# An MLP on one core: the residual's row of factors moves from the up projection to the down projection's first block

## The chip, the cores and the metric

The kernel runs on one core of a Trainium2 chip. The metric is the device time of one execution in microseconds. Engines: TensorE (PE) multiplies, VectorE (DVE), ScalarE (ACT) and GpSimd (POOL) work elementwise, SyncE (SP) issues all the DMAs of this kernel, and each of them works through its own queue in order.

## The reference

A decoder layer on 1024 tokens of width 1024: mixing heads, cross attention, then the part that matters here, an MLP with squared ReLU, and a last norm.

```python
u = jax.nn.relu(rmsnorm(x, ln2[l]) @ w_ff1[l])
x = x + (u * u) @ w_ff2[l]
return rmsnorm(x, ln_f)
```

`w_ff1` is 1024 x 4096, `w_ff2` 4096 x 1024. The kernel does not wait for this norm's factor r: it feeds the up projection with x times a factor c of each token that it has already (that of the norm before). Since relu(c a) squared is c squared times relu(a) squared, the MLP comes out too large by (c/r) squared. The last norm does not mind a factor of a whole token, once EPS is scaled too. So it is enough that the residual x is multiplied, token by token, by the same (c/r) squared, a row of 1024 factors called `inv`, before the down projection's sums are added to it.

## The kernel before, in words

Everything is held transposed: features on the 128 partitions, the 1024 tokens along the free axis, in two halves of 512. Each product of two fp32 numbers is made as three fp32r products (lines 184, 185, 186 in `mm3`) of a high part (`wh`, made by ScalarE, line 132) and a low part (`wl`, made by VectorE, line 133). TensorE's work in the MLP is two block algorithms of Strassen's kind, with seven products (numbers 1 to 7) instead of eight.

*Up projection* (about 880 to 1215 us of the profile). A list of jobs, one product of 12 matmuls each, runs over 16 pairs of tiles of `w_ff1`. A job takes a bank of PSUM from a cycle of eight, and the next job on the same bank waits until VectorE has added the sum to what stands in SBUF (line 1326). The squared results are combined and stored to DRAM (`right`, lines 1366 and 1367; `plain` for the last block). Between the jobs, by their number `at`: at 30 the factors `inv` are turned into a row (`to_row`: a transpose on TensorE, line 247, a copy by ScalarE, 248, a store to DRAM, 249, and a load that spreads it over all partitions, 251), in the constant tile `row`. From 32 on, every fourth job calls `stretch`: in turns it loads a 128x1024 piece of the residual from DRAM (`x2d`, line 1427) into a buffer `w4`, or multiplies that piece by `row` on VectorE (1430) and stores it back (1431). There are eight pieces. The last pairs of jobs use the halves of `row` as scratch afterwards. The tag `w4` has five buffers of 128x1024, shared by the pairs' partial results, the stretches and later by the down projection's split weights.

*Down projection* (about 1215 to 1500 us). 7 blocks of 4 steps, `(b, m)`. A step has seven products of 6 matmuls, on four banks: products 2, 4 and 3 go on in the banks of 1, 5 and 7, after VectorE has added those to the residual's tile `x2` (line 1517). `left` loads the raw weights of the next step (1403), GpSimd makes sums of them (1410), and ScalarE and VectorE split both (132, 133; the split of 128x768 goes to two `w4` buffers, that of 128x1024 to `wh` and `wl`). The residual's tiles are loaded once, tile m before or during step m - 1 of the first block (`x2_load`, 1476: 1 MB each), stay in SBUF over all blocks, and are prepared on GpSimd by two subtractions (`distances`, 1490).

The order of the instructions on every engine is set by a scheduler that plays the program through with costs of its own, so a change of dependences and buffers moves instructions.

Of the kernel before, what the change touches and what calls it, by code (L numbers as in the profile page):

```python
# [12 lines left out]
ALU = mybir.AluOpType  # L13
# [8 lines left out]
KT = D // P  # L22
# [22 lines left out]
def hybrid_layer(ctx: ExitStack, tc: tile.TileContext, a: dict, out: bass.AP):  # L45
    nc = tc.nc
    v, s, g = nc.vector, nc.scalar, nc.gpsimd
# [11 lines left out]
    def sb(tag, shape, bufs, dt=F32):  # L59
        return pool.tile(shape, dt, tag=tag, name=name(tag), bufs=bufs)  # L60

    def act(dt=F32R):
        return sb("act", [P, 8, TH], 7, dt)
# [8 lines left out]
    def w4(shape=(P, 1024), dt=F32):  # L72
        t = sb("w4", [P, 1024], 5, dt)[: shape[0]]
        return t.rearrange("p (a b) -> p a b", b=shape[2]) if len(shape) == 3 else t
# [33 lines left out]
    def const(n, shape, dt=F32):  # L108
        return pool.tile(shape, dt, tag=n, name=n, bufs=1)

    load = nc.sync.dma_start
# [76 lines left out]
    def both(pair, f):  # L188
        return f(pair[0]), f(pair[1])
# [52 lines left out]
    rowd = dram.tile([4, T], F32, name="rowd")  # L242

    def to_row(dst, cols, n, at, bank=None):

        ps = (bank or ov_)()
        nc.tensor.transpose(ps[:n, :P], cols, ident)
        s.activation(dst[:n, :P], ps[:n, :P], AF.Copy)
        load(at.rearrange("o (t q) -> (o t) q", t=n), dst[:n, :P])
        w = min(dst.shape[1], n * P)  # L250
        return load(dst, at[:, :w].broadcast_to([P, w]))

    row = const("row", [P, T])
# [12 lines left out]
    at = 0  # L266
# [33 lines left out]
    h = [(act(), act()), (act(), act())]  # L300
# [20 lines left out]
    for k in range(KT):  # L321
        if k == 2:
            load(wg_raw, a["w_gate"])
        if k % 2 == 0:
            c = slice(k % 4 * 256, k % 4 * 256 + 512)
# [354 lines left out]
    for _ in range(2):  # L680
        t = act().rearrange("p a b -> p (a b)").rearrange("p (i c) -> p i c", i=4)
# [363 lines left out]
    n = 0  # L1045
# [7 lines left out]
    for step in fill:  # L1053
        n, e = divmod(halves[0], 2)
# [82 lines left out]
    x2d = dram.tile([P, KT // 2, 2, 2, TH], F32, name="x2d")  # L1137
# [23 lines left out]
    def bank():  # L1161
        turn[0] += 1
        return ps_tile(cycle[turn[0] % 8])
# [63 lines left out]
    def prepare(at):  # L1227
        while prep and first[prep[0]] <= at + LEAD:
            left_up(*prep.pop(0))
# [10 lines left out]
    inv = gcol.rearrange("p a b -> p (a b)")[:, :8]  # L1240
# [10 lines left out]
    def norm_factors(hf):  # L1251

        ps = bank()
        sum_cols(ps[:, 0:4], accs[hf], 4)
        c = slice(4 * hf, 4 * hf + 4)
        v.tensor_scalar(out=inv[:, c], in0=ps[:, 0:4], scalar1=1.0 / D, scalar2=EPS, op0=ALU.mult, op1=ALU.add)
        for _ in range(2):
            v.tensor_tensor(out=inv[:, c], in0=inv[:, c], in1=rcol[:, c], op=ALU.mult)
# [110 lines left out]
    def put_right(b, k, pair):  # L1369

        u11, u12, u21, u22 = (pair.u[c] for c in ("11", "12", "21", "22"))
        t1 = pair.t1
        to = lambda c: [right[b][ORDER.index(c), :, p_, k] for p_ in range(2)]
        t = {}

        def one():
            sub(t1, u12, u11)
            put(to("11"), u11)

        def two():  # L1380
            x = w4()
            t[2], t[4] = x[:, :TH], x[:, TH:]
            sub(t[2], u22, t1)
            sub(u12, u22, u12, g)
            put(to("t1"), t1)

        def four():
            sub(t[4], t[2], u21)
            put(to("22"), u22)

        return [one, two, lambda: put(to("t3"), u12), four, lambda: put(to("21"), u21), lambda: put(to("t2"), t[2]), lambda: put(to("t4"), t[4])]

    def put_plain(k, pair):
        f = lambda i, hf: lambda: put([plain[2 * i + k, :, p_, hf] for p_ in range(2)], pair.u[f"{i + 1}{hf + 1}"])
        return [f(i, hf) for hf in range(2) for i in range(2)]
# [4 lines left out]
    def left(src):  # L1400

        q = sb("wr", [P, 1024], 2)
        after[0] = load(q, src)
        q = q.rearrange("p (q c) -> p q c", q=4)
        q21, q11, q12, q22 = (q[:, i] for i in range(4))
        sums = z4()[:, :1024].rearrange("p (q c) -> p q c", q=4)
        s1, s2, s3, s4 = (sums[:, i] for i in range(4))

        for o, x, y, op in ((s1, q21, q22, ALU.add), (s2, s1, q11, ALU.subtract), (s3, q11, q21, ALU.subtract), (s4, s2, q12, ALU.subtract)):
            g.tensor_tensor(out=o, in0=x, in1=y, op=op)  # L1410
        hq, lq = (w4(dt=F32R)[:, :768].rearrange("p (q c) -> p q c", q=3) for _ in range(2))
        split(hq, lq, q[:, 1:])
        hs, ls = (sb(t, [P, 1024], 3, F32R).rearrange("p (q c) -> p q c", q=4) for t in ("wh", "wl"))
        split(hs, ls, sums)
        f = lambda hi, lo, i: both((hi, lo), lambda t: t[:, i].rearrange("p (k c) -> p k c", k=2))
        return {1: f(hq, lq, 0), 2: f(hq, lq, 1), 3: f(hs, ls, 3), 4: f(hq, lq, 2), 5: f(hs, ls, 0), 6: f(hs, ls, 1), 7: f(hs, ls, 2)}

    stretches = list(range(KT))

    held = []  # L1420

    def stretch(n):

        x = x2d[:, n // 2, n % 2].rearrange("p h c -> p (h c)")
        if not held:
            held.append(w4())
            load(held[0], x)
        else:
            t = held.pop()
            v.tensor_tensor(out=t, in0=t, in1=row, op=ALU.mult)  # L1430
            load(x, t)

    pairs = {}
    later = []
    for at, (p_, i) in enumerate(jobs):
        prepare(at)
        for _ in range(2 if at < 2 else 1):
            if rest and at:
                rest.pop(0)()
        if at == 6:  # L1440
            norm_factors(1)
        if at == 30:
            to_row(row, inv, 8, rowd[3:4], bank)
        if at > 30 and at % 4 == 0 and stretches:
            stretch(stretches[0])
            if at % 8 == 4:
                stretches.pop(0)
        if at == len(jobs) - 3:
            lefts = left(a["w_ff2q"][0, 0])
        if later:  # L1450
            later.pop(0)()
        pair = pairs.setdefault(p_, Pair(p_))
        pair.run(i, cuts.pop((p_, i)))
        if i == 4:
            b, k = todo[p_][:2]
            later += put_right(b, k, pair) if b < NB - 1 else put_plain(k, pair)
            del pairs[p_]
# [5 lines left out]
    def rights(b, at):  # L1463

        t = act()
        n = min(2, 7 - at)
        for e in range(n):
            load(t[:, 4 * e : 4 * e + 4].bitcast(F32), right[b][at + e].rearrange("p e k c -> p (e k) c"))
        return {SEVEN[at + e]: (t[:, 4 * e : 4 * e + 2], t[:, 4 * e + 2 : 4 * e + 4]) for e in range(n)}

    x2 = []

    def x2_load(m):
        if m % 2 == 0:
            x2.append(act(F32).rearrange("p (m i h) c -> p m i h c", m=2, i=2))
        load(x2[m // 2][:, m % 2], x2d[:, m])
# [6 lines left out]
    r.update(rights(0, 4))  # L1483
    r.update(rights(0, 6))

    def distances(op, m):

        x = x2[m // 2][:, m % 2]
        for i, hf in ((0, 1), (1, 0)):
            g.tensor_tensor(out=x[:, i, hf], in0=x[:, i, hf], in1=x[:, 1, 1], op=op)  # L1490

    for at, (b, m) in enumerate(steps):
        now = lefts
        if m == 0:
            r_now, r = r, {}
        if at + 1 < len(steps):
            b1, m1 = steps[at + 1]
            lefts = left(a["w_ff2q"][b1, m1])
        with tc.issue_after(after[0].ins):
            if at < 3:  # L1500
                x2_load(at + 1)
            if b + 1 < NB - 1:
                for i in ((), (), (0,), (2, 4, 6))[m]:
                    r.update(rights(b + 1, i))
        if b == 0:
            distances(ALU.subtract, m)
        x = x2[m // 2][:, m % 2]
        x11, x12, x21, x22 = (x[:, i, j] for i in range(2) for j in range(2))
        held = {}

        for i, of, y, op in ((1, 1, x22, ALU.add), (5, 5, x22, ALU.add), (7, 7, x22, ALU.add), (6, 6, x22, ALU.add), (2, 1, x11, ALU.add), (4, 5, x21, ALU.subtract), (3, 7, x12, ALU.subtract)):
            if of == i:
                held[of] = bank()
            ps = held[of]
            for k in range(2):
                mm3(ps, both(now[i], lambda t: t[:, k]), both(r_now[i], lambda t: t[:, k]), of == i and k == 0, k == 1, True)
            v.tensor_tensor(out=y, in0=y, in1=ps, op=op)
        if b == NB - 2:
            distances(ALU.add, m)

# [2 lines left out]
    for i in range(2):  # L1523
        t = act()
# [105 lines left out]
```

## Time and profile before

| | us |
|---|---|
| time, median of 3 runs | 1556.06 (1556.05 to 1556.83) |
| span of the profiled execution, from its first to its last instruction | 1551.3 |
| mean granted TensorE clock in it | 0.994 |
| TensorE busy | 1512.5 |
| VectorE busy | 1115.3 |
| DMA | 311.9 MB, 57.7% of 16 engines' span |

The profile gives the profiled execution's own time only as its span; the runs' times are 4.8 us above it. Times in the views count from the span's start. `PE ... [2.78 <-DVE r_f L1326]` reads: TensorE was idle for 2.78 us before this instruction, until VectorE's instruction of line 1326 that writes `r_f` was done. A row of busy time by stages gives for each engine the busy us and, in brackets, the number of instructions, then the granted clock of TensorE, the share of the DMA engines' time, and GB/s.

### The profile page before, as it was taken

The numbers are of one execution on the slowest core, as the hardware profiler recorded it, in microseconds if no ns is written. First come the engines' busy times: TensorE is split into PE (matmuls) and PEld (weight loads), VectorE is DVE, ScalarE is ACT, GpSimd is POOL, SyncE is SP. The second block draws the span as 40 slices with busy tenths as digits, with TensorE's granted clock in tenths as the row PEclk, the third lists the DMA queues.
The fourth block names the chain that finished last, engine by engine and source line by source line (L and its number), as shares of the span: only waits on it lengthen the run. The fifth ranks groups of instructions, "written<-read, shape, count | busy, mean of one in ns | idle before, by whom it ended". The sixth has DMA issues, their size and how long they took to land. (4 is left out here: it accounts for less than half of the span.)

```text
span 1551.3 us, 22016 instructions
## 1 busy us (share of the span) xinstructions
PE 1512.5 (97%) x7729; PEld 1262.4 (81%) x7729; DVE 1115.3 (72%) x1736; ACT 721.7 (47%) x1351; POOL 474.4 (31%) x515
## 2 busy tenths in 40 slices
PE   8999999999999999999999999989999999999997
PEld 8878888889898887788888787777777878888887
DVE  7666676665789874944457988888877777767666
ACT  7324343334787763634443556556555422211234
POOL 0003030413455441511110034444444633333320
PEclk9999999999999999999999999999999999999998
DMA  6422223436878949943344457777777976666623
GB/s 220 122 78 84 99 99 113 130 130 170 253 252 231 296 165 312 321 156 117 115 156 154 145 178 265 277 276 260 269 251 261 387 288 244 238 245 239 243 93 110
DMA packets 122108, 311.94 MB, mean 201 GB/s; under 512 B 13566, under 2 KB 28216, under 8 KB 114060
## 3 DMA queue, kind: packets, MB, share of 16 engines
q1 hardware_dynamic: 121996, 310.52, 57.7%
q8 instruction: 61, 1.00, 0.3%
q14 instruction: 51, 0.42, 0.1%
HBM read 206.42 MB, written 104.05 MB: 200 GB/s over the span
## 5 line engine op out<-in xcount | busy, mean ns | idle before, releaser
L184 PE MATMUL tp<-act,wl 128*128 128x512 f32 (+1 forms) x448 | 177.5, 396 | 6.9 <-DVE r_f L1326 3.8
L185 PE MATMUL tp<-act,wh 128*128 128x512 f32 (+1 forms) x448 | 176.3, 393 | 0.0
L186 PE MATMUL tp<-act,wh 128*128 128x512 f32 (+1 forms) x448 | 175.9, 394 | 0.0
L133 DVE TENSOR_TENSOR wl<-wr,wh 128x1024 fp32r<-128x1024 f32 (+2 forms) x99 | 129.1, 1304 | 27.4 <-ACT wh L132 27.0
L132 ACT ACTIVATE wh<-wr 128x1024 fp32r<-128x1024 f32 (+2 forms) x99 | 99.0, 1000 | 86.8 <-PE tp L186 37.2
L184 PE MATMUL mm<-act,wl 128*128 128x512 f32 (+1 forms) x336 | 130.7, 389 | 3.0 <-DVE r_e L1071 1.5
L186 PE MATMUL mm<-act,wh 128*128 128x512 f32 (+1 forms) x336 | 129.0, 384 | 0.0
L185 PE MATMUL mm<-act,wh 128*128 128x512 f32 (+1 forms) x336 | 128.8, 383 | 0.0
L184 PE MATMUL m<-act,wl 128*128 128x512 f32 (+1 forms) x312 | 120.5, 386 | 1.8 <-DVE wl L133 1.5
L186 PE MATMUL m<-act,wh 128*128 128x512 f32 (+1 forms) x312 | 119.3, 382 | 0.0
L185 PE MATMUL m<-act,wh 128*128 128x512 f32 (+1 forms) x312 | 119.1, 382 | 0.0
L184 PEld LDWEIGHTS tp<-act,wl 128*128 128x128 f32 x448 | 84.7, 189 | 28.0 <-DVE r_f L1326 4.2
L184 PE MATMUL sc<-act,wl 128*128 128x512 f32 (+1 forms) x252 | 99.2, 394 | 5.3 <-DVE r_f L1326 3.4
L186 PEld LDWEIGHTS tp<-act,wh 128*128 128x128 f32 x448 | 84.7, 189 | 19.5
L1410 POOL TENSOR_TENSOR z<-wr 128x256 f32<-128x256 f32 x56 | 50.7, 924 | 161.9 <-DMA wr<-w_ff2q 146.2
L185 PEld LDWEIGHTS tp<-act,wh 128*128 128x128 f32 x448 | 84.8, 189 | 18.8
L132 ACT ACTIVATE w<-wr 128x768 fp32r<-128x768 f32 (+2 forms) x31 | 25.6, 826 | 157.5 <-PE tp L186 90.1
L185 PE MATMUL sc<-act,wh 128*128 128x512 f32 (+1 forms) x252 | 98.5, 391 | 0.0
L186 PE MATMUL sc<-act,wh 128*128 128x512 f32 (+1 forms) x252 | 98.3, 390 | 0.0
L132 ACT ACTIVATE wh<-z 128x1024 fp32r<-128x1024 f32 (+1 forms) x54 | 55.4, 1027 | 56.0 <-POOL z L1410 22.2
L133 DVE TENSOR_TENSOR wl<-z,wh 128x1024 fp32r<-128x1024 f32 (+1 forms) x54 | 73.5, 1362 | 6.1 <-ACT wh L132 5.9
L184 PEld LDWEIGHTS mm<-act,wl 128*128 128x128 f32 x336 | 63.3, 188 | 16.9 <-DVE r_e L1071 1.9
(676 smaller groups left out, 4242.1 us busy)
## 6 DMA issues: line engine op xcount, KB each, us to landing
act<-right SPq DMA_DIRECT2D x49, 1024.0 KB
right<-w SPq DMA_DIRECT2D x56, 256.0 KB
wr<-w_ff2q SPq DMA_DIRECT2D x28, 512.0 KB
right<-r_d SPq DMA_DIRECT2D x49, 256.0 KB
right<-r_e SPq DMA_DIRECT2D x49, 256.0 KB
act<-fqk SPq DMA_DIRECT2D x48, 256.0 KB
wr<-w_in SPq DMA_DIRECT2D x20, 512.0 KB
wr<-w_ff SPq DMA_DIRECT2D x20, 512.0 KB
```

The costliest lines, as they stand in the source:

```text
L132: s.activation(hi, src, AF.Copy)
L133: return v.tensor_tensor(out=lo, in0=src, in1=hi.bitcast(F32), op=ALU.subtract)
L184: nc.tensor.matmul(ps, w[1], x[0], start=first, stop=False, skip_group_check=more)
L185: nc.tensor.matmul(ps, w[0], x[1], start=False, stop=False, skip_group_check=more)
L186: nc.tensor.matmul(ps, w[0], x[0], start=False, stop=last, skip_group_check=more)
L1410: g.tensor_tensor(out=o, in0=x, in1=y, op=op)
```

## The change

The eight pieces no longer go through SBUF and back to DRAM in the up projection. The row of factors goes to a `w4` buffer of its own, `by_norms`, which is held from the up projection until the fourth tile of the residual is scaled. Each tile of `x2` is multiplied by it in place, in two instructions of 128x1024 on VectorE (`scaled`), after it is loaded and before its `distances`: tile 0 ahead of the first step, tile m + 1 behind the second product of step m.

```diff
-    stretches = list(range(KT))
-
-    held = []
-
-    def stretch(n):
-
-        x = x2d[:, n // 2, n % 2].rearrange("p h c -> p (h c)")
-        if not held:
-            held.append(w4())
-            load(held[0], x)
-        else:
-            t = held.pop()
-            v.tensor_tensor(out=t, in0=t, in1=row, op=ALU.mult)
-            load(x, t)
+    by_norms = w4()
...
         if at == 30:
-            to_row(row, inv, 8, rowd[3:4], bank)
-        if at > 30 and at % 4 == 0 and stretches:
-            stretch(stretches[0])
-            if at % 8 == 4:
-                stretches.pop(0)
+            to_row(by_norms, inv, 8, rowd[3:4], bank)
...
+    def scaled(m):
+
+        for i in range(2):
+            x = x2[m // 2][:, m % 2, i].rearrange("p h c -> p (h c)")
+            v.tensor_tensor(out=x, in0=x, in1=by_norms, op=ALU.mult)
...
-        if b == 0:
-            distances(ALU.subtract, m)
+        if at == 0:
+            scaled(0)
+            distances(ALU.subtract, 0)
...
             v.tensor_tensor(out=y, in0=y, in1=ps, op=op)
+            if at < 3 and i == 5:
+                scaled(at + 1)
+                distances(ALU.subtract, at + 1)
```

Lines behind line 1418 have other numbers in the changed kernel: `left` keeps 1403 and 1410, the multiplications in `scaled` are line 1473, the load of x2's tiles is 1459, the adds of the down projection are 1507.

VectorE in the up projection, around the eighth stretch, before (`r_f`, `r_p`, `w` are a pair's partial results, `ov` and the like are banks):

```order
L133 TENSOR_TENSOR w_1993_11129<-w_1993_11129,r_d_11480 128x512
L133 TENSOR_TENSOR r_f_11176<-r_f_11176,r_e_11459 128x512
L1430 TENSOR_TENSOR w_2027_11350<-w_2027_11350,row 128x1024
L1326 TENSOR_TENSOR r_p_11069<-ov_11163,r_p_11069 128x512
L133 TENSOR_TENSOR r_c_11277<-wr_11269,r_b_11276 128x512
```

The same place now:

```order
L133 TENSOR_TENSOR w_1988_11106<-w_1988_11106,r_d_11449 128x512
L133 TENSOR_TENSOR r_f_11151<-r_f_11151,r_e_11428 128x512
L1326 TENSOR_TENSOR r_p_11046<-ov_11138,r_p_11046 128x512
L133 TENSOR_TENSOR r_c_11250<-wr_11242,r_b_11249 128x512
L1166 TENSOR_TENSOR w_2028_11388<-w_2028_11388,r_p_11046 128x512
```

Only line 1430 is gone from here; SP's two instructions for it are gone from SP's queue.

VectorE at the passage, before: the last adds of the up projection (1326) and the splits for the first steps of the down projection.

```order
L1326 TENSOR_TENSOR r_f_11755<-sc_11701,r_f_11755 128x512
L133 TENSOR_TENSOR wl_11853<-z_2094_11843,wh_11852 128x1024
L1326 TENSOR_TENSOR r_f_11778<-mm_11721,r_f_11778 128x512
L1326 TENSOR_TENSOR w_2079_11714<-tp_11742,w_2079_11714 128x512
L133 TENSOR_TENSOR wl_11976<-z_2115_11966,wh_11975 128x1024
L1326 TENSOR_TENSOR w_2082_11734<-sc_11765,w_2082_11734 128x512
```

The same place now (`act` is the tile of x2 that holds tiles 0 and 1, `w_1717` is `by_norms`):

```order
L1326 TENSOR_TENSOR r_f_11724<-sc_11670,r_f_11724 128x512
L1473 TENSOR_TENSOR act_11926<-act_11926,w_1717_9217 128x1024 x2
L133 TENSOR_TENSOR wl_11822<-z_2087_11812,wh_11821 128x1024
L1326 TENSOR_TENSOR r_f_11747<-mm_11690,r_f_11747 128x512
L1473 TENSOR_TENSOR act_11926<-act_11926,w_1717_9217 128x1024 x2
L1326 TENSOR_TENSOR w_2072_11683<-tp_11711,w_2072_11683 128x512
L133 TENSOR_TENSOR wl_11945<-z_2108_11935,wh_11944 128x1024
L1326 TENSOR_TENSOR w_2075_11703<-sc_11734,w_2075_11703 128x512
```

Four multiplications stand between adds and splits for which TensorE waits.

VectorE in steps 0 and 1 now (1507 are the adds, the split of 128x768 is that of the next step's weights; before, there was no line 1473 here):

```order
L133 TENSOR_TENSOR w_2110_11941<-wr_11933,w_2109_11940 128x768
L1507 TENSOR_TENSOR act_11926<-act_11926,sc_11973 128x512
L1473 TENSOR_TENSOR act_12025<-act_12025,w_1717_9217 128x1024 x2
L1507 TENSOR_TENSOR act_11926<-act_11926,sc_12027 128x512
L133 TENSOR_TENSOR wl_12022<-z_2118_12012,wh_12021 128x1024
L133 TENSOR_TENSOR row<-row,r_e_11905 128x512
L133 TENSOR_TENSOR w_2075_11703<-w_2075_11703,r_e_11915 128x512
L1507 TENSOR_TENSOR act_11926<-act_11926,mm_12035 128x512
L1507 TENSOR_TENSOR act_11926<-act_11926,sc_12027 128x512
L1507 TENSOR_TENSOR act_11926<-act_11926,tp_12047 128x512
L1507 TENSOR_TENSOR act_11926<-act_11926,sc_12055 128x512
L1473 TENSOR_TENSOR act_12025<-act_12025,w_1717_9217 128x1024 x2
```

The third tile's multiplications stand ahead of the first add of step 1, the fourth's ahead of the 128x768 split for step 2, which is the next row.

## The prediction

> **What bounds the kernel now.** I read the page's first line, then busy time by stages, then every idle stretch of TensorE in the MLP, and last the chain behind the longest of them. The page says that TensorE is nearly always busy, so a change off TensorE is worth only the idle time it ends and the slow clock that follows idle time.
>
> ```profile
> PE 1512.5 (97%) x7729; PEld 1262.4 (81%) x7729; DVE 1115.3 (72%) x1736; ACT 721.7 (47%) x1351; POOL 474.4 (31%) x515
> core 0: us, PE busy (x) PEld busy (x) DVE busy (x) ACT busy (x) POOL busy (x), PEclk, DMA share, GB/s
> 880.00:950.00 70.00, 69.26 (x302) 55.57 (x301) 63.37 (x83) 43.46 (x71) 22.20 (x14) 1.00 0.53 185
> 950.00:1190.00 240.00, 227.39 (x950) 180.47 (x948) 198.69 (x217) 146.18 (x230) 112.70 (x69) 0.98 0.74 262
> 1204.00:1242.00 38.00, 38.00 (x164) 30.64 (x163) 27.56 (x36) 17.88 (x26) 22.70 (x20) 1.00 1.02 387
> 1300.00:1500.00 200.00, 200.00 (x859) 161.15 (x858) 138.28 (x181) 38.35 (x41) 71.12 (x76) 1.00 0.59 232
> 1020.40:1023.80 3.40, 3.40 (x9) 2.64 (x10) 3.40 (x4) 2.52 (x5) 2.27 (x2) 0.51 0.78 288
> 1147.80:1153.50 5.70, 5.70 (x13) 4.45 (x14) 4.08 (x5) 2.73 (x5) 4.41 (x3) 0.50 0.55 203
> ```
>
> The row 1300 to 1500 is the down projection at full speed: 859 matmuls in 200 us, 0.2328 us each. At that rate 240 us hold 1031; the row 950 to 1190, the up projection with the eight stretches in it, has 950. The 81 missing ones are 18.8 us. The row 880 to 950, the same loop before the stretches start, loses 0.7 us. Of the 18.8 us, 240.0 - 227.4 = 12.6 are idle; the two short rows, at half clock, lose half of 3.4 and of 5.7, together 4.5; the remaining 1.7 are the edges of eight gaps, 0.2 each.
>
> These are seven of the gaps as TensorE's timeline shows them (the eighth, at 956.76, is 0.62 and has no stretch before it), and behind them VectorE's multiplications by `row` (line 1430), with the load that they wait for:
>
> ```profile
> 978.06 0.50 PE L184 MATMUL sc<-act,wl 128*128 128x512 f32 x1 [1.44 <-DVE wl L133]
> 1020.31 0.67 PE L184 MATMUL sc<-act,wl 128*128 128x512 f32 x1 [2.78 <-DVE r_f L1326]
> 1043.17 0.50 PE L184 MATMUL m<-act,wl 128*128 128x512 f32 x1 [1.46 <-DVE wl L133]
> 1083.21 0.50 PE L184 MATMUL mm<-act,wl 128*128 128x512 f32 x1 [0.59 <-DVE r_f L1326]
> 1104.52 0.50 PE L184 MATMUL tp<-act,wl 128*128 128x512 f32 x1 [1.45 <-DVE wl L133]
> 1147.79 0.79 PE L184 MATMUL tp<-act,wl 128*128 128x512 f32 x1 [3.79 <-DVE r_f L1326]
> 1170.76 0.50 PE L184 MATMUL sc<-act,wl 128*128 128x512 f32 x1 [0.49 <-DVE wl L133]
> ...
> 974.45 1.21 DVE L1430 TENSOR_TENSOR w<-w,row 128x1024 f32<-128x1024 f32 x1
> 1013.91 1.23 DVE L1430 TENSOR_TENSOR w<-w,row 128x1024 f32<-128x1024 f32 x1 [1.23 <-DMA w<-x2d]
> 1039.56 1.22 DVE L1430 TENSOR_TENSOR w<-w,row 128x1024 f32<-128x1024 f32 x1
> 1099.88 2.25 DVE L1430 TENSOR_TENSOR w<-w,row 128x1024 f32<-128x1024 f32 x1
> 1141.41 1.23 DVE L1430 TENSOR_TENSOR w<-w,row 128x1024 f32<-128x1024 f32 x1 [1.78 <-DMA w<-x2d]
> DVE w L1430 <- DMA w<-x2d: 11.1, 5, 3.1
> L1430 DVE TENSOR_TENSOR w<-w,row x8: 1214/1226/2252, 974.5 to 1141.4; 128x1024 f32<-128x1024 f32 x8
> ```
>
> Five gaps of 1.4 us and more each follow a stretch within 3.3 to 6.4 us; the short ones (0.59, 0.49, 0.62) do not. The last two rows are from the waits and from the view of line 1430: VectorE stood 11.1 us in all, with a stretch at the head of its queue, for that stretch's load, and the multiplication took 1.23 us at the median and 2.25 at most. The chain in order of time shows how one such wait reaches TensorE:
>
> ```profile
> 1135.88 5.51 DMA w<-x2d
> 1141.41 1.23 DVE w L1430
> ...
> 1147.14 0.61 DVE r_f L1326
> 1147.79 0.79 PE tp L184
> ```
>
> VectorE works in order, so the add of line 1326 that frees the bank comes later by the wait and by the multiplication.
>
> **What leaves the up projection.** For each of the five gaps I take away VectorE's wait and its operation: 978: 1.44 - 1.21 leaves 0.23; 1020: 2.78 - 2.46 leaves 0.32; 1043: 1.46 - 1.22 leaves 0.24; 1104: 1.45 - 2.25 leaves nothing; 1147: 3.79 - 3.01 leaves 0.78. So of 10.9 us idle 9.3 go. With the two long gaps under 1 us their slow clock should go too (the 0.98 of the 240 us is these two and nothing else): 4.5. Five edges of 0.2: 1.0. Sum 14.8 us. Bounds: without the clock part and with half of the gaps' gain, 5; with everything but the stretch-free rate (0.74 in 70 us, so 2.5 in 240), 16.3. I take 14.8, since what is late next, the add of line 1326 without a stretch ahead of it, is in the rows with 0.59.
>
> The sixteen transfers (8.4 of 311.9 MB) I cost at nothing: the DMA engines are 74% busy there. TensorE's transpose and ScalarE's copy of the factors stay, one each. Their two DMAs (lines 249, 251) now stand behind each other in SP's queue, 30 ScalarE instructions later than now, because `by_norms` waits for a `w4` buffer; SP then holds the stores behind them for a landing. Bounds 0 and one more gap of 1.45; I take 0.3. One of five `w4` buffers is held until the second step of the down projection. The stretches used that fifth one in turns before, so in the up projection I cost it at nothing; at the passage it is in the next term.
>
> **What the passage into the down projection gets.** Eight multiplications of 128x1024, the same shape as line 1430, so 1.21 to 2.25 us each, 9.7 to 18.0 in all, go into VectorE's queue between about 1204 and 1242 (times of before). VectorE is busy 27.6 of these 38 us, so 10.4 are free, and TensorE has no idle time there at all, so nothing can be won. The rows that decide:
>
> ```profile
> 1204.07 0.68 DVE L1326 TENSOR_TENSOR r_f<-sc,r_f 128x512 f32<-128x512 f32 x1
> 1206.56 1.92 DVE L133 TENSOR_TENSOR wl<-z,wh 128x1024 fp32r<-128x1024 f32 x1 [1.82 <-ACT wh L132]
> 1211.47 1.23 DVE L133 TENSOR_TENSOR wl<-z,wh 128x1024 fp32r<-128x1024 f32 x1 [1.78 <-ACT wh L132]
> 1218.44 0.69 DVE L1326 TENSOR_TENSOR row<-sc,row 128x512 f32<-128x512 f32 x1 [1.97 <-PE sc L186]
> 1226.61 0.97 DVE L133 TENSOR_TENSOR w<-wr,w 128x768 fp32r<-128x768 f32 x1 [0.24 <-PE tp L184]
> ...
> L1490 POOLq EVENT_SEMAPHORE  x2: 17/17/17, 1204.2 to 1227.0; - x2
> L1490 POOL TENSOR_TENSOR act<-act x16: 1286/1296/2296, 1206.1 to 1494.1; 128x512 f32<-128x512 f32 x16
> 1206.10 3.55 POOL L1490 TENSOR_TENSOR act<-act 128x512 f32<-128x512 f32 x2
> 1237.83 3.27 POOL L1490 TENSOR_TENSOR act<-act 128x512 f32<-128x512 f32 x2 [0.30 <-DMA act<-x2d]
> ```
>
> GpSimd's subtractions (line 1490) tell when x2's tiles land: the first at 1204.2, the third at 1227.0, the fourth at 1237.8.
>
> *First two tiles* (four multiplications, 4.9 to 9.0 us). They stand right behind the add of 1204.07, when the first tile has just landed, ahead of the splits and adds down to the one of 1218.44. The three waits in these rows, 1.8 + 1.8 + 2.0 = 5.6 us, are the cover. Left over: 0 to 3.4; I take 1.0, since half of the multiplications should meet GpSimd (22.7 of 38 us busy).
>
> *Third tile.* It stands between the last add of step 0 and the first of step 1, behind the split of 1226.61. Its work, 2.4 us, delays the add that frees the bank for the product two places later; one other product of 6 x 0.2328 = 1.4 us covers most of it. Cost 0 to 2.4; I take 0.9. The split itself now needs a `w4` buffer that step 0's products hold (four are left, not five), and so does its ScalarE half: 0.5, bounds 0 and 1.8.
>
> *Fourth tile.* Its load is issued behind the raw weights, and these behind the split that ends at 1227.58; it landed at 1237.83, 10.3 us later. VectorE then multiplies 2.4 us and splits 0.97 us, in this order, before TensorE can start step 2's product of that split: 13.7 us. From the same moment TensorE has 48 matmuls ahead of that product (counted in its order), 11.2 us, and loses 0.9 on the way. Stall 1.6; bounds 0 and 5 (each multiplication at 2.25 and the landing 1 us later).
>
> Sum 4.0, bounds 0 and 7.6 + 2.9 = 10.5: the second is 18.0 less the free 10.4, and one slow clock like that of 1147.80. [...]
>
> **The sum.** -14.8 + 0.3 + 4.0 = -10.5 us. The profiled execution has a span of 1551.3; the median of the runs is 1556.06, 4.8 us around the span, which I keep. Forecast: span 1540.8, time 1545.6, 0.7% faster. No change that can be measured is within 0.2%, 3.1 us.
>
> **The rivals.**
> - *The passage costs nothing*: -14.5, so 1541.5. For it: VectorE idles 10.4 us there and waits for TensorE, not the reverse. Against: the fourth tile lands too late for its place. 0.20.
> - *Every multiplication meets GpSimd.* All eight take 2.25 and VectorE is 7.6 us over its free time: 1556.1 - 14.5 + 7.6 = 1549.2. For it: GpSimd's four subtractions per pair of tiles grow from 1.3 to 1.8 us each at 1206.10 beside VectorE; against: seven of the eight take 1.24 or less now, as their median says. 0.12. [...]
> - *The gaps close only in part*: what fills VectorE's freed time is the next late add. Half of the gaps' gain and one of the slow clocks: about -7 + 4.3, so 1553.4, within 0.2%. For it: 0.59 at 1083 comes without a stretch. Against: the row 880 to 950. 0.13.
> - *Slower*: the multiplications stand at the head of VectorE's queue for loads that land when the DMA engines are full (share 1.02). If the third and fourth tile land 6 us later than now, TensorE stops twice for some 6 us and loses 2.9 at half clock after each, as at 1147.80: 2 x 8.9, or 17.7, on top of 1.0 for the first two: 1556.1 - 14.5 + 18.7 = 1560.3. It decides from about 4.5 us later on. For it: landing takes 9 us and more already. Against: the two loads keep their places behind the same weights, up to two stores, and the DMA engines carry no more than before. 0.12.
>
> The forecast has 0.43. Faster: 0.43 + 0.20 + 0.12 = 0.75; within 0.2%: 0.13; slower: 0.12. The range 1540 to 1554.5 leaves out the slower rival and a few in a hundred on each side; the forecast's own range is 1542.5 to 1549.
>
> **What would show it.** TensorE's gaps from 950 to 1190 under 1 us each and no slow clock there; its busy row there some 15 us shorter for the same matmuls. Waits for x2's tiles by VectorE in the passage, of which the fourth is the longest; new TensorE gaps of 0.5 to 3 us between the last jobs of the up projection and step 2. I am wrong if gaps of over 1 us stay behind line 1326 without a stretch, or if a gap of over 2.8 us opens in the passage.

## The result, and the profile after

The changed kernel takes 1542.24 us (median of four runs, 1541.6 to 1545.24), the kernel before 1556.05 in the same comparison: a ratio of 0.9916, with a 95% interval of 0.99 to 0.9931. That is 0.8% faster; forecast were 0.7% and 1545.6 us.

The line of busy time on the changed kernel's page:

```profile
PE 1508.6 (98%) x7729; PEld 1259.3 (82%) x7729; DVE 1125.5 (73%) x1736; ACT 722.5 (47%) x1351; POOL 480.0 (31%) x515
```

Its busy time by stages, in the columns shown for the kernel before (PE, PEld, DVE, ACT, POOL, then granted clock, DMA share, GB/s):

```profile
950.00:1190.00 240.00, 238.31 (x1017) 190.38 (x1016) 210.09 (x226) 151.84 (x236) 120.81 (x76) 1.00 0.72 249
1190.00:1240.00 50.00, 46.40 (x194) 35.66 (x193) 47.92 (x53) 19.95 (x29) 31.59 (x27) 1.00 0.93 338
1240.00:1300.00 60.00, 60.00 (x258) 48.32 (x257) 43.24 (x57) 12.70 (x14) 20.48 (x25) 1.00 0.71 280
```

The last two stages of the kernel before (the first has its row in the prediction, 950 matmuls):

```profile
1190.00:1240.00 50.00, 50.00 (x216) 40.29 (x215) 39.00 (x49) 22.55 (x34) 28.55 (x26) 1.00 1.01 374
1240.00:1300.00 60.00, 59.12 (x254) 47.16 (x253) 44.95 (x59) 13.27 (x14) 21.96 (x29) 1.00 0.68 263
```

Count the matmuls, at 0.2328 us each. From 950 to 1190 there are 67 more: 15.6 us gained. From 1190 to 1240 there are 22 fewer: 5.1 us lost. From 1240 to 1300 there are 4 more: 0.9 won back. The net is 11.4 us; the two spans, 1551.3 and 1540.1, differ by 11.2. The granted clock of the up projection is 1.00, not 0.98.

All of TensorE's gaps from 950 to 1190 that the timeline shows, and behind the "..." those of the passage into the down projection:

```profile
977.11 0.50 PE L184 MATMUL sc<-act,wl 128*128 128x512 f32 x1 [0.31 <-DVE wl L133]
1036.57 0.50 PE L184 MATMUL m<-act,wl 128*128 128x512 f32 x1 [0.31 <-DVE wl L133]
1096.12 0.50 PE L184 MATMUL tp<-act,wl 128*128 128x512 f32 x1 [0.50 <-DVE wl L133]
1155.68 0.50 PE L184 MATMUL sc<-act,wl 128*128 128x512 f32 x1 [0.50 <-DVE wl L133]
...
1199.83 0.50 PE L184 MATMUL tp<-act,r_c 128*128 128x512 f32 x1 [0.50 <-DVE w L1326]
1214.74 0.50 PE L184 MATMUL sc<-act,w 128*128 128x512 f32 x1 [0.64 <-DVE w L133]
1218.20 0.50 PE L184 MATMUL sc<-act,w 128*128 128x512 f32 x1 [0.41 <-DVE act L1507]
1220.11 0.50 PE L184 MATMUL tp<-act,wl 128*128 128x512 f32 x1 [0.25 <-DVE wl L133]
1228.60 0.50 PE L184 MATMUL m<-act,w 128*128 128x512 f32 x1 [1.23 <-DVE w L133]
1230.83 0.50 PE L184 MATMUL mm<-act,wl 128*128 128x512 f32 x1 [0.57 <-DVE wl L133]
```

The five long gaps are gone, and so are the two slow clocks. The six new gaps all end with an operation of VectorE, and VectorE is busy 47.92 of the 50 us; it has no idle moment right ahead of any of the six operations. What it does ahead of the longest of them, from its timeline:

```profile
1224.72 0.69 DVE L1507 TENSOR_TENSOR act<-act,sc 128x512 f32<-128x512 f32 x1
1225.32 2.35 DVE L1473 TENSOR_TENSOR act<-act,w 128x1024 f32<-128x1024 f32 x2
1227.59 0.95 DVE L133 TENSOR_TENSOR w<-wr,w 128x768 fp32r<-128x768 f32 x1
```

The view of the line of the multiplications (1473), with their durations in ns:

```profile
L1473 DVE TENSOR_TENSOR act<-act,w x8: 1210/1220/2307, 1190.1 to 1226.5; 128x1024 f32<-128x1024 f32 x8
its engine sat idle before it (us, times) until:
who waited for it (us, times):
  POOL act L1479: 7.7, 3
```

Nothing stands under "its engine sat idle": in the changed kernel VectorE never waited for a tile of x2. The fourth tile's two multiplications began when VectorE came to them, without an idle moment ahead, and the split that TensorE needed stood behind them.

### The profile page after: what moved, and what is told of

It is laid out like the page before. It is cut to its first block, busy times and chain, and to the rows that moved or that the text cites. A ratio compares the mean times of both kernels' runs of the same rounds, so it can differ in the third digit from the quotient of the medians.

```text
span 1540.1 us, 22015 instructions
## 1 busy us (share of the span) xinstructions
PE 1508.6 (98%) x7729; PEld 1259.3 (82%) x7729; DVE 1125.5 (73%) x1736; ACT 722.5 (47%) x1351; POOL 480.0 (31%) x515
```

## The experiments

The theory: in the up projection, VectorE's waits and multiplications of line 1430 held TensorE; at the passage, the multiplications hold it from their places in VectorE's queue. The rivals: the traffic through DRAM, the place of the `w4` buffers, or the landing of x2's tiles. The medians of one and the same kernel move by up to 1.2 us here (1555.1 to 1556.29 for the kernel before, 1541.62 and 1542.24 for the changed one), so the matmul counts of a stage are read beside them.

### The up projection without the stretches

```diff
-        if at > 30 and at % 4 == 0 and stretches:
+        if False and at % 4 == 0 and stretches:
```

> The kernel before without load, multiplication and store of the eight tiles in the up projection (lines 1427, 1430 and 1431); the residual is added unscaled, so a part of the computation is left out. Theory (the stretches held VectorE, and VectorE held TensorE): the five long gaps and both slow clocks between 950 and 1190 us go, nothing is paid at the passage into the down projection, and the time falls by the prediction's up projection term of 14.8 us, or by the 16.4 us that the spacing of the matmuls in the two traces gives: 1539 to 1541.5 beside 1556. Rival (the gain came with the other place of the w4 buffers and of the order, not with the stretches): under 5 us gained, 1551 or more.

Measured: 1540.23 us, ratio 0.9904 (0.9886 to 0.9922), the kernel before at 1555.26. 1014 matmuls in the 240 us where the kernel before has 950 and the changed kernel 1017:

```profile
950.00:1190.00 240.00, 237.54 (x1014) 189.96 (x1013) 208.68 (x225) 152.13 (x236) 121.11 (x75) 1.00 0.71 248
1190.00:1240.00 50.00, 49.93 (x215) 39.79 (x214) 36.77 (x49) 21.57 (x30) 27.02 (x28) 1.00 1.00 387
```

The stretches are 64 of the stage's 81 missing matmuls; the other 17 stay, with five gaps of 0.31 to 0.66 us. With no multiplication at the passage nothing is lost there. There is no `by_norms` in this kernel, so the other place of that buffer is not what gained; the buffers of the stretches are free here too, and the next run keeps them in use.

### The transfers without the multiplication

```diff
             t = held.pop()
-            v.tensor_tensor(out=t, in0=t, in1=row, op=ALU.mult)
             load(x, t)
```

> The kernel before with the sixteen transfers of the stretches at their old places and without the multiplication of line 1430 between them; the residual is added unscaled, so a part of the computation is left out. Theory (VectorE's wait for the load at the head of its queue and the multiplication are the cost, the transfers themselves are not): nearly all of the gain stays, 1539 to 1543. Rival (8.4 MB less through DRAM, or SyncE's queue freed of the store's wait, is what gained): the time stays within 3 us of 1556, and TensorE keeps gaps of 1 us and more behind the five places.

Measured: 1539.9 us, 0.9901 (0.9883 to 0.992).

```profile
950.00:1190.00 240.00, 237.07 (x1012) 189.48 (x1011) 207.68 (x224) 152.13 (x237) 120.01 (x75) 1.00 0.81 282
```

The DMA engines are busier here than before the change (0.81 against 0.74), the eight loads stand where they stood in SyncE's queue and the stores a few places from there at most, and TensorE loses two matmuls against the run without them. The 8.4 MB and SyncE's queue cost nothing that can be seen.

### The multiplication without a load to wait for

```diff
-            held.append(w4())
-            load(held[0], x)
+            held.append(None)
...
-            t = held.pop()
-            v.tensor_tensor(out=t, in0=t, in1=row, op=ALU.mult)
-            load(x, t)
+            held.pop()
+            t = w4()
+            v.tensor_tensor(out=t, in0=row, in1=row, op=ALU.mult)
```

> The kernel before with eight multiplications of 128x1024 at the old places of the stretches, but of the row of factors with itself, so that they wait for no load; no transfer, and the residual is added unscaled, so a part of the computation is left out. If the work of line 1430 (10.8 us of VectorE in all) holds TensorE, half of the gain or more is lost and some of the five gaps stay: 1547 or more. If the wait for the load (11.1 us in all) is what made the gaps, the gaps stay under 1 us, no slow clock follows, and the time is 1540 to 1544.

Measured: 1543.84 us (1542.69 to 1545.53), 0.9931 (0.9913 to 0.9949). The time falls where the second case was, the trace does not: gaps and one slow clock stay. The stage, and the 3.4 us behind the longest gap:

```profile
950.00:1190.00 240.00, 232.56 (x980) 184.11 (x979) 213.51 (x223) 147.27 (x231) 115.93 (x70) 0.99 0.68 237
1141.30:1144.70 3.40, 3.40 (x8) 2.70 (x9) 3.40 (x4) 2.51 (x5) 2.20 (x2) 0.52 0.77 285
```

TensorE's two longest gaps there, from its timeline:

```profile
1079.20 0.50 PE L184 MATMUL mm<-act,wl 128*128 128x512 f32 x1 [1.43 <-DVE r_f L1326]
1141.29 0.69 PE L184 MATMUL tp<-act,wl 128*128 128x512 f32 x1 [1.91 <-DVE r_f L1326]
```

980 matmuls lie between 950 and 1014, so work and wait share the loss. By the medians the wait for the load is the larger part, 11.4 us (1555.26 - 1543.84), and the work 3.6 (1543.84 - 1540.23); by this profile, that of the longest of the four runs, it is 7.0 and 7.9 us (30 and 34 matmuls). The order of VectorE's instructions differs a little too, and the eight multiplications take 12.7 us here and 10.8 in the kernel before, so the shares are rough; that both count is shown.

### The changed kernel without its multiplications

```diff
         for i in range(2):
             x = x2[m // 2][:, m % 2, i].rearrange("p h c -> p (h c)")
-            v.tensor_tensor(out=x, in0=x, in1=by_norms, op=ALU.mult)
+            pass
```

> The changed kernel without the eight multiplications of line 1473; the residual is added unscaled, so a part of the computation is left out. Theory (VectorE's queue at the passage is the whole cost of the new place): the gaps of 0.4 to 1.2 us between 1199 and 1231 us go, 4 to 4.6 us, and the time is 1537.5 to 1538.5 beside 1542.2 for the changed kernel, with the span under 1537. Rival (the gaps come from the loads of x2's tiles and from the w4 buffer that step 0's products hold, which stay): TensorE keeps at least 2 us of gaps there and the time is 1540 or more.

Measured: 1538.06 us (1536.41 to 1539.8), 0.9891 (0.9868 to 0.9913), 4.2 us under the changed kernel. The profiled span is 1537.5, a little above what I had expected.

```profile
1190.00:1240.00 50.00, 50.00 (x215) 40.16 (x214) 36.78 (x50) 21.38 (x30) 28.59 (x28) 1.00 1.01 386
1240.00:1300.00 60.00, 59.48 (x255) 47.42 (x254) 41.99 (x57) 11.35 (x12) 18.72 (x24) 1.00 0.64 252
```

215 matmuls where the changed kernel has 194: no gap is left in these 50 us, although x2's loads stay. One thing goes with the multiplications, other than I had expected: nothing reads `by_norms` any more, so its `w4` buffer is free again after its load, and other tiles use it in the up projection and at the passage. So the passage's cost is the multiplications and the held buffer together. For the multiplications speaks that VectorE in the changed kernel never stood idle right ahead of an operation that ended a gap, as it would if that operation had waited for a free buffer; the run with the fourth tile alone moved, below, holds the buffer longer and has fewer gaps.

### Only the first two tiles' multiplications

```diff
-            v.tensor_tensor(out=x, in0=x, in1=by_norms, op=ALU.mult)
+            if m < 2:
+                v.tensor_tensor(out=x, in0=x, in1=by_norms, op=ALU.mult)
```

> The changed kernel with the multiplications of tiles 0 and 1 alone; tiles 2 and 3 are added unscaled, so a part of the computation is left out. If the cost of the passage is the sum of what each pair of multiplications leaves over, the gaps at 1199 and 1214 us stay (1.5 us by the spacing of the matmuls) and those from 1218 to 1231 us, 3.1 us, go: 1539 to 1540, between 1538.1 without any multiplication and 1542.2 with all. If VectorE's queue has room for four and not for eight (its backlog is one, and it breaks only with the late ones), nothing is lost and the time is 1538.1, with no gap over 0.3 us from 1195 to 1235.

Measured: 1539.83 us (1539.03 to 1541.92), 0.9903 (0.9886 to 0.992); between the other two, as the first case had it. The passage, and then the gaps from 1195 to 1235:

```profile
1190.00:1240.00 50.00, 48.84 (x208) 38.33 (x207) 43.48 (x51) 19.93 (x29) 31.00 (x27) 1.00 0.98 370
```

```profile
1202.72 0.50 PE L184 MATMUL tp<-act,r_c 128*128 128x512 f32 x1 [0.59 <-DVE w L1326]
1231.70 0.50 PE L184 MATMUL mm<-act,wl 128*128 128x512 f32 x1 [0.57 <-DVE wl L133]
```

208 matmuls: without the second pair of tiles 14 of the 21 lost ones come back, 3.3 us, and 7, or 1.6 us, stay lost. But the gaps are not the ones I named. That of 1214 is gone. One of 0.57 at 1231, ended by the split `wl`, stays with no multiplication near it: GpSimd's subtractions for the fourth tile run there (1227.30 to 1230.57), and the split takes 1.71 us beside them where it takes 1.21 in the run without multiplications. VectorE also waits 0.8 us for the first tile here, which it does not in the changed kernel. So 1.6 us is not the price of the first pair's multiplications alone.

### Three tiles later

```diff
-            v.tensor_tensor(out=y, in0=y, in1=ps, op=op)
+            added = v.tensor_tensor(out=y, in0=y, in1=ps, op=op)
             if at < 3 and i == 5:
-                scaled(at + 1)
+                with tc.issue_after(added.ins):
+                    scaled(at + 1)
                 distances(ALU.subtract, at + 1)
```

> The changed kernel in which the multiplications of tiles 1, 2 and 3 are issued behind the add of product 5 of the step before, so that they move later in VectorE's order: tile 1 behind the first adds of step 0, tile 2 into step 1, tile 3 into step 2; everything is computed. Theory (VectorE is busy without a break from 1189 to 1230 us, and spreading its work over the emptier time behind it ends the gaps): 1 to 3 us of the 4.2 are won back, 1539 to 1541. Rival (each pair of multiplications costs its place wherever it stands, as long as adds and splits wait behind it): no gain, 1542 to 1543, with the gaps moved to 1210 to 1250 us.

Measured: 1543.47 us (1541.58 to 1544.84), 0.9927 (0.9914 to 0.994): nothing won, 0.5 us over the rival's 1542 to 1543. VectorE's timeline, and TensorE's behind it:

```profile
1219.35 0.68 DVE L1507 TENSOR_TENSOR act<-act,mm 128x512 f32<-128x512 f32 x1
1219.95 3.19 DVE L1473 TENSOR_TENSOR act<-act,w 128x1024 f32<-128x1024 f32 x2
1223.06 1.21 DVE L133 TENSOR_TENSOR wl<-z,wh 128x1024 fp32r<-128x1024 f32 x1
...
1224.33 0.50 PE L184 MATMUL tp<-act,wl 128*128 128x512 f32 x1 [2.59 <-DVE wl L133]
1224.67 0.39 PE L185 MATMUL tp<-act,wh 128*128 128x512 f32 x1
...
1225.15 0.63 PE L184 MATMUL tp<-act,wl 128*128 128x512 f32 x1
...
1228.54 0.39 PE L186 MATMUL sc<-act,wh 128*128 128x512 f32 x1
```

The third tile now stands right ahead of the split `wl` for which TensorE waits: a gap of 2.59, and then eight matmuls of 0.43 us from start to start. The fourth tile, moved into step 2, has no gap near it, and the one of 1199 is gone; two of 0.36 and 0.95 us stand at 1212 and 1215. So the place in the queue decides, not only how much VectorE has to do.

### The last two tiles on GpSimd

```diff
-            v.tensor_tensor(out=x, in0=x, in1=by_norms, op=ALU.mult)
+            (v if m < 2 else g).tensor_tensor(out=x, in0=x, in1=by_norms, op=ALU.mult)
```

> The changed kernel with the multiplications of tiles 2 and 3 on GpSimd; everything is computed. GpSimd is busy 31.6 of the 50 us at the passage, and four such operations should take some 2.6 us each there, twice its 1.29 for half the elements. Theory (VectorE's queue is the cost, not the landing of the loads): the gaps from 1218 to 1231 us go, and the time is 1539 to 1540.5. Rival (GpSimd's sums of the weights for steps 2 and 3 stand behind the multiplications and come late, or VectorE's own operations are held while GpSimd multiplies): new gaps of 2 us and more behind VectorE's splits of z, and 1543 or more.

Measured: 1542.41 us (1540.17 to 1544.42), 0.9921 (0.9905 to 0.9937): as the changed kernel. From the timelines: GpSimd's multiplications and its subtractions behind them, two of VectorE's operations beside them, and TensorE's last two gaps:

```profile
1215.34 4.87 POOL L1473 TENSOR_TENSOR act<-act,w 128x1024 f32<-128x1024 f32 x2 [0.60 <-DMA act<-x2d]
1220.28 3.85 POOL L1479 TENSOR_TENSOR act<-act 128x512 f32<-128x512 f32 x2
...
1218.70 2.58 DVE L133 TENSOR_TENSOR wl<-z,wh 128x1024 fp32r<-128x1024 f32 x1
1221.21 1.78 DVE L133 TENSOR_TENSOR row<-row,r_e 128x512 fp32r<-128x512 f32 x1
...
1229.43 0.50 PE L184 MATMUL m<-act,w 128*128 128x512 f32 x1 [0.84 <-DVE act L1507]
1236.08 0.50 PE L184 MATMUL mm<-act,wl 128*128 128x512 f32 x1 [0.67 <-DVE wl L133]
```

The gaps of 1218 and 1220 are gone and the long one is 0.84 us, but the one ended by the split `wl` has grown to 0.67. VectorE's split of 128x1024 took 2.58 us beside GpSimd, 1.98 in the changed kernel and 1.22 in the run without multiplications. The one of 128x512 behind it took 1.78, as in the changed kernel (1.77), and 0.69 without multiplications. The slower operations of the rival are there, though they cost less than it said: part of what leaves VectorE's queue, 0.6 us at this split, comes back as slower operations. What else eats the gain, these rows do not show.

### The kernel before, profiled again

> The kernel before, unchanged, for another profile. Its executions lie between 1551.8 and 1557.1 us. If the late loads of the stretches are what varies, the wait of VectorE for them, the gaps behind it and the slow clocks differ from the first profile (span 1551.3), and the stretch from 950 to 1190 us holds another number of matmuls than 950; the rest of the span stays. If not, the difference lies outside the up projection, and 1.7 us lie around the span, as in the runs of the changed kernel.

Measured: 1554.23 us, span 1552.5. The up projection, and then its two longest gaps:

```profile
950.00:1190.00 240.00, 226.74 (x949) 180.16 (x948) 198.98 (x217) 145.98 (x228) 112.21 (x69) 0.98 0.74 262
```

```profile
1020.90 0.79 PE L184 MATMUL sc<-act,wl 128*128 128x512 f32 x1 [2.90 <-DVE r_f L1326]
1148.50 0.80 PE L184 MATMUL tp<-act,wl 128*128 128x512 f32 x1 [3.86 <-DVE r_f L1326]
```

The up projection is the same to one matmul, with both slow clocks: its loss is no chance of one execution. The span is 1.2 us longer, and the matmul counts put that at the passage: 213 and 251 from 1190 to 1240 and to 1300, against 216 and 254. 1.7 us lie around the span, and 1.7 to 1.9 in every run that lists its span. Over the 28 executions of the kernel before in these comparisons the spans go from 1549.6 to 1557.3 us, with a mean granted clock of 0.995 in the eight shortest, and 0.992 in the longest. On the whole the longer ones have more of the slow clock; where it lies, no profile shows.

### Fewer tiles later

Tile 3 (the fourth) alone, behind the add of product 5 of step 2:

```diff
-            v.tensor_tensor(out=y, in0=y, in1=ps, op=op)
-            if at < 3 and i == 5:
+            added = v.tensor_tensor(out=y, in0=y, in1=ps, op=op)
+            if at < 2 and i == 5:
...
+            if at == 2 and i == 5:
+                with tc.issue_after(added.ins):
+                    scaled(3)
+                distances(ALU.subtract, 3)
```

> The changed kernel with the multiplications of tile 3 alone issued later, behind the add of product 5 of step 2, where they cost nothing when three tiles were moved. Theory: the gaps of 1.23 and 0.57 us at 1228 and 1230 us go, those of tiles 1 and 2 stay, 1540 to 1541. Rival (the split for step 2 is late for another reason, the landing of its weights or the backlog of the adds): the gap of 1.23 us stays and the time is 1542.

Tile 3 in that way, and tile 2 behind the add of product 7 of step 1:

```diff
-            if at < 3 and i == 5:
+            if at == 0 and i == 5:
...
+            if (at, i) in ((1, 7), (2, 5)):
+                with tc.issue_after(added.ins):
+                    scaled(at + 1)
+                distances(ALU.subtract, at + 1)
```

> The changed kernel with the multiplications of tile 2 issued behind the add of product 7 of step 1, and those of tile 3 behind the add of product 5 of step 2; tile 1 stays. In VectorE's order tile 2 then stands behind the split of the sums for step 1 and tile 3 behind that for step 2, where in the run with three tiles moved tile 2 stood right ahead of such a split and cost 2.59 us and a slow clock. Theory (a multiplication costs TensorE what it delays the next split or add that TensorE needs, so its place among those decides, not its number): the gaps of 1218 to 1231 us, 3.1 us, shrink to about 1, and the time is 1539.5 to 1541 beside the changed kernel on the same chip at 1542. Rival (VectorE's work at the passage is simply too much): 1542 or more, with the gaps at other places.

And the changed kernel beside them:

> The changed kernel, unchanged, on the same chip as the other two of this call: 1541.5 to 1543.5 by its four runs (one of them 1545.2), 1.7 us of which lie around the span. The gaps from 1199 to 1231 us are there again, 4 to 5 us in all, if VectorE's backlog makes them and not one execution's chance.

Measured, on one chip with the kernel before at 1556.29: the fourth tile alone 1540.21 (1540.0 to 1541.68; 0.9896, 0.9881 to 0.9911), both 1542.54 (1541.6 to 1543.41; 0.9908, 0.9892 to 0.9923), the changed kernel 1541.62 (1540.9 to 1543.01; 0.9905, 0.9892 to 0.9919). With the fourth tile alone moved, TensorE has 204 matmuls in the 50 us, and from 1190 to 1300 the gaps of the second fence and no others:

```profile
1190.00:1240.00 50.00, 48.48 (x204) 37.80 (x203) 48.04 (x54) 19.51 (x29) 30.05 (x25) 1.00 0.89 327
```

```profile
1201.51 0.50 PE L184 MATMUL tp<-act,r_c 128*128 128x512 f32 x1 [0.59 <-DVE w L1326]
1216.05 0.50 PE L184 MATMUL sc<-act,w 128*128 128x512 f32 x1 [0.25 <-DVE w L133]
1219.57 0.50 PE L184 MATMUL sc<-act,w 128*128 128x512 f32 x1 [0.45 <-DVE act L1507]
1221.46 0.50 PE L184 MATMUL tp<-act,wl 128*128 128x512 f32 x1 [0.23 <-DVE wl L133]
```

The gaps of 1228 and 1230 are gone, ten matmuls or 2.3 us are back in the window, and VectorE is as busy as in the changed kernel (48.04 and 47.92): not how much VectorE does, but what stands behind it. The edit moves GpSimd's subtractions for that tile as well, since they wait for the multiplications. The gap of 1228 ended with a split of 0.95 us that is as long here (0.96), so it was the multiplications'. The split that ended the one of 1230 took 1.72 us beside the subtractions and takes 1.22 here; with the same gap in the run of the first two tiles, it is the subtractions' at least in part. SyncE's queue has every load in the place that it has in the changed kernel, so the landing of the weights or of x2 did not make those gaps. In the run of the changed kernel they are there again (1.24 and 0.56). With both tiles moved the adds behind tile 2 come late, and gaps of 0.84 and 0.53 stand where the old ones went: the rival's time.

The fourth tile alone is the fastest kernel here that computes everything: 1.4 us, or 0.1%, under the changed kernel by the medians. That is less than the bound of 0.2% by which a difference is called measured, so only the gaps speak for it.

## Why the prediction was right, and where it was not

- **The up projection, -14.8.** Right, and a little small: 67 matmuls are 15.6 us. I had left gaps of 0.6 without a stretch ahead of them and 0.8 of the longest; the one at 1083 went too (0.28 of it stays in one run), though the last stretch ahead of it lies 25 us back; how it hangs on the stretches is not shown. Four gaps that a split ends stay, at 0.3 to 0.5. That both of the long gaps take their slow clock with them is shown by the 1.00.
- **Transfers at nothing.** Shown: 1539.9 with and 1540.23 without them.
- **The row's DMAs behind each other, +0.3.** No gap of the changed kernel from 950 to 1190 follows anything but a split, so it is nothing that can be seen.
- **The passage, +4.0.** Right as a sum: 5.1 us less 0.9 by the counts, and 4.2 by the kernel without multiplications (which frees the `w4` buffer as well). Its parts can't be told so finely: 1.0 for the first two tiles and 3.0 for the rest were forecast, and the run with only the first two tiles gives 1.6 and 3.3, the 1.6 with a wait and a slowed split in it. The shortage of `w4` buffers, 0.5, was not seen: VectorE was not idle ahead of any operation that ended a gap. I had not counted that the splits slow down beside the subtractions that now follow each multiplication: the one of `wl` behind the third tile takes 1.98 us, and 1.22 in the run without multiplications.
- **The fourth tile.** The step "its load is issued behind the raw weights ... 10.3 us later" failed as a cause. VectorE waited for no tile; it was late itself, busy without a break behind the adds of step 1, and reached the fourth tile later than its load. That 1.6 us were near 1.23 and 0.57 of idle time was luck: the run with that tile moved has the same load at the same place and neither gap.
- **The time around the span, 4.8.** The step "which I keep" failed, and it is most of the miss of 3.4 us. 1.7 us lie around the span; the other 3.1 were the distance from one of the shorter executions of the kernel before (span 1551.3) to the median. With 1.7 the forecast span of 1540.8 gives 1542.5, and 1542.24 was measured. The other side of it: by the medians the change gained 13.8 us, where the sum has 10.5 and the two profiled spans differ by 11.2. So in the longer executions of the kernel before the change took away some 3 us that no term of the sum names; which stage they lie in stays open.
- **The rivals.** The time alone does not decide: 1542.24 lies just under the forecast's own range (1542.5 to 1549), and nearer to the 1541.5 of *The passage costs nothing*. That rival falls with the 21 matmuls that the passage lost. *Every multiplication meets GpSimd*: some do, up to 2.31 us each, but the median is 1.22. *The gaps close only in part*: none over 0.5 stayed. *Slower*: VectorE waited for no load in the changed kernel (once in each of two variants, for 0.8 and 0.5 us), and no gap at the passage passed 1.23.
- **What would show it.** The gaps under 1 us, the clock and the 15 us are as said; new gaps of 0.5 to 3 us stand where I put them, with two shorter ones. VectorE's waits for x2's tiles, "of which the fourth is the longest", do not exist.
- **A reading in the working.** The five long gaps follow a stretch within 3.6 to 6.4 us by the rows shown, not 3.3.

## What to carry to other kernels

An operation in VectorE's queue cost here what it delayed the next operation behind it that TensorE waited for. Read that from the order and the waits: a load at the head of the queue counted with its wait (11.1 us of VectorE over five stretches), and a pair of the same multiplications left no gap behind one add, and one of 2.59 us and a slow clock ahead of one split. A saving is summed against the profiled span; what lies around the span, and how far that execution is from the median, are two numbers, and only the first is kept.

## What the runs showed of the hardware

The half clock came with gaps of 1.91 us (the multiplication without a load), 2.59 (three tiles later), 2.78, 2.90, 3.79 and 3.86, and not with those of 1.43 to 1.46. It did not come either with a gap of 1.84 us in the run without stretches, or with this one, ahead of the MLP in the run without multiplications; the second line is the half clock of the kernel before around its gap of 3.79:

```profile
654.15 0.27 PE L247 MATMUL ov<-ident,rcol 128*4 128x128 f32 x1 [1.85 <-DVE rcol L206]
1146.80:1153.60 6.80, 5.81 (x14) 4.55 (x15) 5.18 (x7) 3.73 (x6) 4.51 (x3) 0.50 0.52 193
```

With the gaps of up to 2.90 it lasted some 3.4 us. With those of 3.79 and 3.86 it lasted 6.8, twice that, and its first 1.0 and 1.7 us still lay in the gap. With 2.59 the first three matmuls still ran at full speed (0.34, 0.23 and 0.25 us from start to start, then 0.42). So the longest of these gaps without the half clock is 1.85 us, and the shortest with it 1.91; whether the moment of a gap counts beside its length, no run here settles.

With the last two tiles on GpSimd, two of VectorE's operations with two inputs in SBUF slowed beside GpSimd's, 2.58 us against the 1.22 and 1.78 against the 0.69 of the run without multiplications, the second beside GpSimd's subtractions of line 1479 and not a multiplication. VectorE's adds of line 1507, which take one input from a bank of PSUM, kept 0.67 to 0.69 us in the same stretch.
